# Scan preparation of an RWKV-7 layer with its log decays, normed keys and key factors kept in PSUM

## The chip, the cores and the metric

The kernel runs on one core of a Trainium2 chip. The metric is the device time of one execution in microseconds (us). A core has a matrix engine (TensorE, PE in the profile, with its weight loads as PEld), a vector engine (VectorE, DVE), a scalar engine (ScalarE, ACT), GpSimd (POOL), and SyncE (SP), which issues most DMAs. Matmul results land in PSUM, which is handled here as eight buffers (banks) of 512 fp32 columns on 128 partitions; all other tiles lie in SBUF. Each engine works through its own queue in order.

## The reference

Two sequences (256 and 1024 tokens, together T = 1280) run through two layers of width 1024. Layer 0 is a bidirectional RWKV-7 time mixer with 16 heads of 64, layer 1 neighbourhood attention; each is followed by a squared-ReLU MLP. The change touches only the inputs of the scan of layer 0:

```python
kk = _heads((k * k_k).astype(f32))
kk = kk * lax.rsqrt(jnp.maximum(jnp.sum(jnp.square(kk), axis=-1, keepdims=True), L2_EPS))
for d in range(2):
    w_lora = jnp.tanh(xw @ w1[d]) @ w2[d]
    decay = jnp.exp(-jnp.exp(-jax.nn.softplus(-(w0[d] + w_lora).astype(f32)) - 0.5))
    iclr = _heads(jax.nn.sigmoid((a0[d] + (xa @ a1[d]) @ a2[d]).astype(f32)))
    k_d = kf * (1.0 + (iclr - 1.0) * k_a_h)
    y = y + _wkv_scan(rf, _heads(decay), k_d, vf, -kk, kk * iclr, reverse=(d == 1))
    bonus = bonus + jnp.sum(rf * k_d * r_k, axis=-1, keepdims=True)
```

The log of the decay is -0.6065 times a sigmoid. `_wkv_scan` is computed later in chunks of 64 tokens. For each chunk it needs r, kk, k_d and kk*iclr multiplied by the exponential of the running sum of the log decays, or by its inverse.

## The kernel before

**Stages.** First the projections that give k and a part of r, then the stage of the change (about 315 to 677 us of the execution), then the scan of layer 0, its MLP, the attention layer and its MLP.

**Units.** The preparation has 48 units h: 8 blocks m of 128 channels (two heads), in each three segments of tokens (256, 512 and 512 wide), in each two directions d. So of six units in a row two are 256 wide and four are 512 wide, even units run forward and odd ones backward. For one unit:

- `prep_first` j = 0 and 1: a matmul of the decay's and of the rate's low-rank factors (`l<-tw,wa` and `l<-ta,wa`, L602), each followed by a tanh on ACT (L603), into `lw` and `tha`. j = 2: ACT's affine step makes the log decay of `lw` in place (L596). `lw` has 65 columns a chunk, one of which stays zero.
- `prep_scan`: DVE's scan (L615) sums the log decays within each chunk into `cs`; `prep_exp`: ACT makes exp(cs) and exp(-cs), `ec` and `emc` (L626, L629).
- `prep_keys`, even units only: a matmul spreads the inverse norms of the heads over the channels (`kb`, L675), DVE multiplies with the keys into `pkk` (L678).
- `prep_products`: POOL makes r*ec (L646) and kd*emc (L652); DVE makes the key factor 1+(iclr-1)*k_a out of `tha` (L648), multiplies it with k (L650, `kd`), and makes (tha+1)*kk (L654), -kk*ec (L656) and (tha+1)*kk*emc/2 (L658). L660 takes the decay of a whole chunk out of `ec`.
- `prep_store`: two DMAs on ACT's queue write the products to HBM.
- `prep_bonus`, for each pair of units: DVE multiplies kd with r (L690), PE sums over the head in `bps` (two columns a block of 128 tokens, L694), DVE copies that out (L696).

**Other work in the stage.** PE also projects the rest of r: 18 bursts of 24 matmuls into `rps` (L95 to L97, called from `rmm`), one for every two units from unit 7 on, evacuated by ACT. From unit 42 on it projects v (`vps`, L499 to L501), whose inputs are loaded and cast tile by tile (`vx`, `mh`, L430 and L431) from unit 39 on.

**Order.** The order of the compute engines is written out by hand: `at(t, f, ...)` puts a step at a time t, counted in units; the list is sorted by t and all is issued in that order, so that each engine's queue follows it. For unit h the matmul of `tw` stands at h-2.027, that of `ta` at h-2.13, the affine step at h-1.765, the scan at h-0.95, the products at h+0.084 to h+0.57, the bonus steps of an even unit at h+2.58, h+4.45 and h+5.824.

**PSUM.** Three buffers (`pa`) serve `rps` and `vps`; four (pool `ppl`, tag `l2`) are handed out in turn to the two matmuls of `prep_first` and to `kb`; one (pool `ppn`) is for `bps`. A matmul into a buffer waits until the last reader of what stood there is done.

Of the kernel before, what the change touches and what calls it, by code (L numbers as in the profile page):

```python
# [13 lines left out]
P = 128  # L14
# [4 lines left out]
L = 64  # L19
# [29 lines left out]
class Trunk:  # L49
# [50 lines left out]
    def l0_proj(self):  # L100
# [410 lines left out]
    def prep_open(self, bctx):  # L511
        nc, tc, a = self.nc, self.tc, self.a
        self.ar_d = self.dram("ar_d", [8, 2, P, 20, P])
        self.bk_d = self.dram("bk_d", [8, 2, P, 20, P])
        pp = self.pp = bctx.enter_context(tc.tile_pool(name="ppB", bufs=1, reuse_waits="tile", side="right"))
        self.pk = bctx.enter_context(tc.tile_pool(name="pkB", bufs=2, reuse_waits="tile", side="right"))
        self.ppl = bctx.enter_context(tc.tile_pool(name="plB", bufs=4, space=PSUM))
        self.ppn = bctx.enter_context(tc.tile_pool(name="pnB", bufs=1, space=PSUM))
        s = self.pre = {}
        for nm in ("tw", "ta"):  # L520
            s[nm] = pp.tile([P, T], F32, name=nm)

# [6 lines left out]
        nc.sync.dma_start(s["m65"], a["m65"])  # L529
        s["hw"] = pp.tile([P, 48], F32, name="hw")  # L530
        s["kr"] = pp.tile([96, 512], F32, name="kr")
        s["heads"] = pp.tile([96, 1024], F32, name="heads")
        nc.sync.dma_start(s["heads"], a["heads"][0:96])
        for i, (c0, c1) in enumerate(SEGS):
            nc.sync.dma_start(s["kr"][32 * i:32 * i + 16, :c1 - c0], self.scr["kr_d"][:, c0:c1])

    def prep_const(self):
        nc, s = self.nc, self.pre
        for d in range(2):
            for t in s["lw"][d]:  # L540
                nc.gpsimd.memset(t[:, :, 64 * d:64 * d + 1], 0.0)
# [45 lines left out]
    def prep_first(self, U, h, j):  # L587

        nc, pk, s, u = self.nc, self.pk, self.pre, U[h]
        m, d, c0, c1, w = self.prep_unit(h)  # L590
        c3 = lambda t: t[:, :w].rearrange("p (c j) -> p c j", j=L)
        lw = u["lw"] = s["lw"][d][h // 2 % 2]
        lv = lw[:, :w // L, 1 - d:65 - d]
        dr = slice(64 * d, 64 * d + 64)
        if j == 2:
            nc.scalar.activation(lv, lv, AF.Copy, scale=-0.5 * KAPPA, bias=-0.5 * KAPPA)  # L596
# [5 lines left out]
        nc.tensor.matmul(ps[:, :w], s["wa", m][dr, j, :], s[act][dr, c0:c1], start=True, stop=True)  # L602
        nc.scalar.activation(t, c3(ps), AF.Tanh, scale=0.5, bias=s["hw"][:, col + 8 * d + m:col + 8 * d + m + 1])  # L603

    def prep_scan(self, U, h):

        nc, pk, s, u = self.nc, self.pk, self.pre, U[h]
        m, d, c0, c1, w = self.prep_unit(h)
        nch = w // L
        flat = lambda t: t[:, :nch, :].rearrange("p c j -> p (c j)")  # L610
        cs = pk.tile([P, 8, 65], F32, name="cs", tag="cs")
        lf, cf = flat(u["lw"]), flat(cs)
        if d == 1:
            lf, cf = lf[:, ::-1], cf[:, ::-1]
        nc.vector.tensor_tensor_scan(out=cf, data0=s["m65"][:, :nch * 65], data1=lf, initial=0.0, op0=ALU.mult, op1=ALU.add)  # L615
        u["cs"] = cs

    def prep_exp(self, U, h, j):
        nc, pk, u = self.nc, self.pk, U[h]
        m, d, c0, c1, w = self.prep_unit(h)  # L620
        nch = w // L
        flat = lambda t: t[:, :nch, :].rearrange("p c j -> p (c j)")
        cs = u["cs"]
        if j == 0:
            ec = u["ec"] = pk.tile([P, 8, 65], F32, name="ec", tag="ec")
            nc.scalar.activation(flat(ec), flat(cs), AF.Exp)  # L626
        else:
            emc = u["emc"] = pk.tile([P, 512], F32, name="emc", tag="emc")
            nc.scalar.activation(emc[:, :w].rearrange("p (c j) -> p c j", j=L), cs[:, :nch, 1 - d:65 - d], AF.Exp, scale=-1.0)  # L629

    def prep_products(self, U, h, i):
        nc, pk, s, u = self.nc, self.pk, self.pre, U[h]
# [5 lines left out]
        tha, emc, ec = u["tha"][:, :w], c3(u["emc"][:, :w]), u["ec"]  # L638
# [6 lines left out]
        if i == 0:  # L645
            nc.gpsimd.tensor_tensor(out=ar[:, :nch, 64:128], in0=c3(r), in1=ec[:, :nch, 1 - d:65 - d], op=ALU.mult)  # L646
        elif i == 1:
            nc.vector.tensor_scalar(out=kd, in0=tha, scalar1=hw[:, 32 + m:33 + m], scalar2=hw[:, 40 + m:41 + m], op0=ALU.mult, op1=ALU.add)  # L648
        elif i == 2:
            nc.vector.tensor_tensor(out=kd, in0=kd, in1=k, op=ALU.mult)  # L650
        elif i == 3:
            nc.gpsimd.tensor_tensor(out=bk[:, :nch, 64:128], in0=c3(kd), in1=emc, op=ALU.mult)  # L652
        elif i == 4:
            nc.vector.scalar_tensor_tensor(out=tha, in0=tha, scalar=1.0, in1=kk, op0=ALU.add, op1=ALU.mult)  # L654
        elif i == 5:
            nc.vector.scalar_tensor_tensor(out=ar[:, :nch, 0:64], in0=c3(kk), scalar=-1.0, in1=ec[:, :nch, d:64 + d], op0=ALU.mult, op1=ALU.mult)  # L656
        elif i == 6:
            nc.vector.scalar_tensor_tensor(out=bk[:, :nch, 0:64], in0=c3(tha), scalar=0.5, in1=emc, op0=ALU.mult, op1=ALU.mult)  # L658
# [7 lines left out]
    def prep_keys(self, U, h, step):  # L666
# [4 lines left out]
            u["kk"] = U[h - 1]["kk"]  # L671
        elif step == 0:
            o = 32 * (h % 6 // 2)
            u["kb"] = self.ppl.tile([P, 512], F32, name="kb", tag="l2")
            nc.tensor.matmul(u["kb"][:, :w], s["heads"][o:o + 16, m * P:m * P + P], s["kr"][o:o + 16, :w], start=True, stop=True)  # L675
        else:
            u["kk"] = self.pk.tile([P, 512], F32, name="pkk", tag="pkk", bufs=2)
            nc.vector.scalar_tensor_tensor(out=u["kk"][:, :w], in0=u["k"][:, :w], scalar=self.v(V_KK, m), in1=u["kb"][:, :w], op0=ALU.mult, op1=ALU.mult)  # L678

    def prep_store(self, U, h, eng):  # L680
# [3 lines left out]
    def prep_bonus(self, U, h, step):  # L684
# [4 lines left out]
            kd = u["kd"][:, :w]  # L689
            nc.vector.scalar_tensor_tensor(out=kd, in0=kd, scalar=self.v(V_RK, m), in1=u["r"][:, :w], op0=ALU.mult, op1=ALU.mult)  # L690
        elif step == 1:
            u["pb"] = self.ppn.tile([P, 8], F32, name="bps", tag="bps")
            for b in range(nb):
                nc.tensor.matmul(u["pb"][:, 2 * b:2 * b + 2], u["kd"][:, b * P:(b + 1) * P], self.blk, start=True, stop=True)  # L694
        else:
# [1181 lines left out]
def host_layout(inputs):  # L1877
# [39 lines left out]
    m65 = np.ones((P, 8, 65), np.float32)  # L1917
    m65[:, :, 0] = 0
    o["lnx"] = np.stack([i["rw_lnx_g"][0].reshape(8, P), i["rw_lnx_b"][0].reshape(8, P)], 1)
    o["m65"] = m65.reshape(P, 520)  # L1920
    return {k: np.ascontiguousarray(v) for k, v in o.items()}


# [17 lines left out]
```

## Time and profile before

| what | value |
|---|---|
| median of 3 runs | 4277.6 us (4269.57 to 4279.12) |
| the profiled execution | 4272.5 us, its span 4270.5 us |
| mean granted clock of TensorE | 0.956 of full |
| busy over the span | PE 94%, DVE 61%, ACT 40%, POOL 37% |
| granted clock in 440 to 480 us | 0.74 |
| busy in 440 to 480 us | PE 37.60, DVE 35.90, ACT 18.70, POOL 26.00 us of 40 |
| granted clock in 1900 to 2000 us (first MLP) | 1.00, PE busy 100 us of 100 |

A busy share is the time in which an engine had an instruction under way. For PE it says little without the granted clock: at 0.50 the same matmul takes twice as long and counts twice. In the rows of a timeline, "x2" are the two records of one fp32 matmul of this stage. Idle time stands in brackets behind an instruction, with what ended it.

### The profile page before, as it was taken

The numbers are of one execution on the slowest core, as the hardware profiler recorded it, in microseconds if no ns is written. First come the engines' busy times: TensorE is split into PE (matmuls) and PEld (weight loads), VectorE is DVE, ScalarE is ACT, GpSimd is POOL, SyncE is SP. The second block draws the span as 40 slices with busy tenths as digits, with TensorE's granted clock in tenths as the row PEclk, the third lists the DMA queues.
The fourth block names the chain that finished last, engine by engine and source line by source line (L and its number), as shares of the span: only waits on it lengthen the run. The fifth ranks groups of instructions, "written<-read, shape, count | busy, mean of one in ns | idle before, by whom it ended". The sixth has DMA issues, their size and how long they took to land.

```text
span 4270.5 us, 69486 instructions
## 1 busy us (share of the span) xinstructions
PE 3994.8 (94%) x25060; PEld 3357.7 (79%) x25060; DVE 2623.4 (61%) x5253; ACT 1716.7 (40%) x4345; POOL 1582.1 (37%) x1877
## 2 busy tenths in 40 slices
PE   7888989888988879999999999999998999999999
PEld 4664658777887768788888888988777788888888
DVE  7888974567877765755555556046554755555555
ACT  6764442366766764211111113256664311111111
POOL 5446664133433353422222225044443422222222
PEclk8996779899999999999999999999999999999999
DMA  3334456566666534111111112535456111111111
GB/s 114 87 108 169 167 172 175 139 160 152 152 159 152 130 96 158 50 35 40 40 40 40 35 35 80 166 101 115 94 119 216 59 35 40 40 40 37 37 37 60
DMA packets 499864, 414.67 MB, mean 97 GB/s; under 512 B 290816, under 2 KB 401312, under 8 KB 499520
## 3 DMA queue, kind: packets, MB, share of 16 engines
q1 hardware_dynamic: 465104, 348.88, 29.5%
q10 hardware_dynamic: 34416, 61.35, 3.9%
q8 instruction: 197, 3.23, 0.3%
q14 instruction: 147, 1.20, 0.1%
HBM read 290.25 MB, written 125.83 MB: 97 GB/s over the span
## 4 chain that ended last, share of the span: by engine, by line
PE 64%; DVE 9%; ACT 3%; DMA 3%; issue 2%; POOL 1%; SPq 1%; ACTq 0%; DVEq 0%; POOLq 0%
PE ps L95 17%; PE ps L96 16%; PE ps L97 16%; DVE tmp L847 2%; DVE q L849 1%; DVE S L1036 1%; PE vps L499 1%; PE vps L501 1%; PE vps L500 1%; PE us L1028 1%; PE aps L807 1%; PE op L1856 1%; PE us L1015 1%; PE w L1006 1%; PE pt L1799 1%
## 5 line engine op out<-in xcount | busy, mean ns | idle before, releaser
L1402 DVE TENSOR_TENSOR x<-ps,x 128x256 f32<-128x256 f32 x1488 | 814.9, 596 | 644.2 <-PE ps L97 644.0
L95 PE MATMUL ps<-ah,whi 128*128 128x512 f32 (+1 forms) x2304 | 843.2, 366 | 0.0
L96 PE MATMUL ps<-al,whi 128*128 128x512 f32 (+1 forms) x2304 | 825.3, 358 | 0.0
L97 PE MATMUL ps<-ah,wlo 128*128 128x512 f32 (+1 forms) x2304 | 822.3, 357 | 1.8 <-DVE wlo L90 1.5
L90 POOL TENSOR_TENSOR wlo<-raw,whi 128x1024 fp32r<-128x1024 f32 (+1 forms) x178 | 390.7, 2195 | 837.3 <-ACT whi L89 833.6
L95 PE MATMUL ps<-hh,whi 128*128 128x512 f32 (+1 forms) x1536 | 547.2, 356 | 9.4 <-DVE x L1402 9.4
L96 PE MATMUL ps<-hl,whi 128*128 128x512 f32 (+1 forms) x1536 | 546.2, 356 | 0.0
L97 PE MATMUL ps<-hh,wlo 128*128 128x512 f32 (+1 forms) x1536 | 545.7, 355 | 0.0
L95 PEld LDWEIGHTS ps<-ah,whi 128*128 128x128 f32 x2304 | 434.3, 189 | 72.0 <-issue 7.8
L97 PEld LDWEIGHTS ps<-ah,wlo 128*128 128x128 f32 x2304 | 433.2, 188 | 72.8 <-DVE wlo L90 2.0
L96 PEld LDWEIGHTS ps<-al,whi 128*128 128x128 f32 x2304 | 434.5, 189 | 62.2 <-issue 1.0
L89 ACT CAST whi<-raw 128x1024 fp32r<-128x1024 f32 (+1 forms) x206 | 200.3, 972 | 703.1 <-PE ps L96 630.1
L1381 POOL TENSOR_TENSOR rl<-rl 128x512 f32<-128x512 f32 (+1 forms) x192 | 173.7, 905 | 505.9 <-PE ps L97 462.4
L1023 POOL COPY u<-hv 64x64 f32<-64x64 f32 x640 | 171.0, 267 | 457.9 <-ACT hv L1017 438.4
L95 PEld LDWEIGHTS ps<-hh,whi 128*128 128x128 f32 x1536 | 291.1, 190 | 53.8 <-DVE x L1402 11.4
L97 PEld LDWEIGHTS ps<-hh,wlo 128*128 128x128 f32 x1536 | 291.4, 190 | 41.7
L1380 ACT ACTIVATE rl<-ps 128x512 f32<-128x512 f32 (+1 forms) x192 | 100.7, 525 | 555.6 <-PE ps L97 555.6
L96 PEld LDWEIGHTS ps<-hl,whi 128*128 128x128 f32 x1536 | 291.1, 190 | 40.6
L1383 ACT CAST hh<-rl 128x512 fp32r<-128x512 f32 (+1 forms) x192 | 105.6, 550 | 324.0 <-POOL rl L1381 324.0
L1036 DVE SCALAR_TENSOR_TENSOR S<-us,dall,sd 64x64 f32<-64x64 f32 x512 | 144.6, 282 | 105.6 <-PE us L1028 97.4
L1384 DVE TENSOR_TENSOR hl<-rl,hh 128x512 fp32r<-128x512 f32 (+1 forms) x192 | 119.8, 624 | 143.2 <-ACT hh L1383 142.5
L1010 ACT COPY u<-w 64x64 f32<-64x64 f32 x640 | 130.8, 204 | 125.6 <-PE w L1006 115.2
(295 smaller groups left out, 8445.4 us busy)
## 6 DMA issues: line engine op xcount, KB each, us to landing
raw<-in_w_down_dram SPq DMA_DIRECT2D x64, 512.0 KB
raw<-in_w_up_dram SPq DMA_DIRECT2D x64, 512.0 KB
ar<-ar_d SPq DMA_DIRECT2D x80, 256.0 KB
bk<-bk_d SPq DMA_DIRECT2D x80, 256.0 KB
ar_d<-ar ACTq DMA_DIRECT2D x32, 512.0 KB
bk_d<-bk ACTq DMA_DIRECT2D x32, 512.0 KB
bs<-tab SPq DMA_DIRECT2D x128, 96.0 KB
v_d<-vt ACTq DMA_DIRECT2D x80, 128.0 KB
```

Of the source, the lines that this page charges most:

```text
L89: nc.scalar.copy(hi[:, cs], raw)
L90: lo_eng.tensor_tensor(out=lo[:, cs], in0=raw, in1=hi[:, cs].bitcast(F32), op=ALU.subtract)
L95: mm(ps, sh, mh, start=first, stop=False)
L96: mm(ps, sh, ml, start=False, stop=False)
L97: mm(ps, sl, mh, start=False, stop=last)
L1010: nc.scalar.copy(up[es, es], w[:64, es])
L1023: nc.gpsimd.tensor_copy(R["u2"][64 * e:64 * e + 64, 64 * e:64 * e + 64], J["hv"][0:64, cc, 64 * e:64 * e + 64])
L1036: nc.vector.scalar_tensor_tensor(out=S2[es, es], in0=sn[es, es], scalar=D, in1=R["sd"][es, es], op0=ALU.mult, op1=ALU.add)
L1381: nc.gpsimd.tensor_tensor(out=r[:, :n], in0=r[:, :n], in1=r[:, :n], op=ALU.mult)
L1383: nc.scalar.copy(hh[:, :n], r[:, :n])
L1384: nc.vector.tensor_tensor(out=hl[:, :n], in0=r[:, :n], in1=hh[:, :n].bitcast(F32), op=ALU.subtract)
L1402: nc.vector.tensor_tensor(out=xv, in0=ps[:, :n], in1=xv, op=ALU.add)
```

## The change

Log decays, the normed keys and the factor out of `ta` stay in PSUM. The matmul for the log decay writes `ltw`, the only buffer of pool `ppn`; tanh and the affine step work on it in place, and the scan reads it there, 64 columns a chunk instead of 65. `ec` takes over the 65th column, set to 1 once, in four lasting tiles. The matmul for the rate writes `lta` (two buffers); ACT puts the tanh into `tha` in SBUF as before, and one more ACT step (Identity with scale and offset) writes the key factor back to `lta`. DVE multiplies that with k, so that step 2 of the products falls away; then (tha+1)*kk overwrites `lta`. `kb` (two buffers) is overwritten with the normed keys and takes the place of `pkk`. `bps` shares the buffer of `ltw`. Four times in the list move: matmul and tanh of `ta` from h-2.13 to h-0.9, the scan from h-0.95 to h-1.2, the second and third bonus step to h+3.83 and h+3.94.

```diff
-            at(lead(-2.13), self.prep_first, U, h, 1)
+            at(lead(-0.9), self.prep_first, U, h, 1)
...
-            at(lead(-0.95), self.prep_scan, U, h)
+            at(lead(-1.2), self.prep_scan, U, h)
...
-                for i, t in enumerate((2.58, 4.45, 5.824)):
+                for i, t in enumerate((2.58, 3.83, 3.94)):
...
-        self.ppl = bctx.enter_context(tc.tile_pool(name="plB", bufs=4, space=PSUM))
+        self.ppl = bctx.enter_context(tc.tile_pool(name="plB", bufs=2, space=PSUM))
         self.ppn = bctx.enter_context(tc.tile_pool(name="pnB", bufs=1, space=PSUM))
...
-        if j == 1:
+        act, col, pool = (("tw", 0, self.ppn), ("ta", 16, self.ppl))[j]
+        ps = pool.tile([P, 512], F32, name="l" + act, tag="l" + act)[:, :w]
+        nc.tensor.matmul(ps, s["wa", m][dr, j, :], s[act][dr, c0:c1], start=True, stop=True)
+        bias = s["hw"][:, col + 8 * d + m:col + 8 * d + m + 1]
+        if j == 0:
+            u["lw"] = ps
+            nc.scalar.activation(ps, ps, AF.Tanh, scale=0.5, bias=bias)
+        else:
+            u["ta"] = ps
             u["tha"] = pk.tile([P, 512], F32, name="tha", tag="tha", bufs=3)
-        act, col, t = (("tw", 0, lv), ("ta", 16, j and c3(u["tha"])))[j]
-        ps = self.ppl.tile([P, 512], F32, name="l2", tag="l2")
-        nc.tensor.matmul(ps[:, :w], s["wa", m][dr, j, :], s[act][dr, c0:c1], start=True, stop=True)
-        nc.scalar.activation(t, c3(ps), AF.Tanh, scale=0.5, bias=s["hw"][:, col + 8 * d + m:col + 8 * d + m + 1])
+            nc.scalar.activation(u["tha"][:, :w], ps, AF.Tanh, scale=0.5, bias=bias)
+            nc.scalar.activation(ps, u["tha"][:, :w], AF.Identity, scale=s["hw"][:, 32 + m:33 + m], bias=s["hw"][:, 40 + m:41 + m])
...
-        nc.vector.tensor_tensor_scan(out=cf, data0=s["m65"][:, :nch * 65], data1=lf, initial=0.0, op0=ALU.mult, op1=ALU.add)
-        u["cs"] = cs
+        nc.vector.tensor_tensor_scan(out=cf, data0=s["m64"][:, :w], data1=lf, initial=0.0, op0=ALU.mult, op1=ALU.add)
...
         elif i == 1:
-            nc.vector.tensor_scalar(out=kd, in0=tha, scalar1=hw[:, 32 + m:33 + m], scalar2=hw[:, 40 + m:41 + m], op0=ALU.mult, op1=ALU.add)
+            nc.vector.tensor_tensor(out=kd, in0=ta, in1=k, op=ALU.mult)
         elif i == 2:
-            nc.vector.tensor_tensor(out=kd, in0=kd, in1=k, op=ALU.mult)
+            return
...
-            nc.vector.scalar_tensor_tensor(out=tha, in0=tha, scalar=1.0, in1=kk, op0=ALU.add, op1=ALU.mult)
+            nc.vector.scalar_tensor_tensor(out=ta, in0=tha, scalar=1.0, in1=kk, op0=ALU.add, op1=ALU.mult)
...
-            u["kk"] = self.pk.tile([P, 512], F32, name="pkk", tag="pkk", bufs=2)
+            u["kk"] = u["kb"]
...
-            u["pb"] = self.ppn.tile([P, 8], F32, name="bps", tag="bps")
+            u["pb"] = self.ppn.tile([P, 512], F32, name="bps", tag="ltw")
```

Two places show how the instructions move. PE, between the burst of `rps` that is 256 wide and the next one, before (`l<-ta` and `l<-tw` are the two matmuls of `prep_first`):

```order
L97 MATMUL rps<-mh_225,wl 128x256
L602 MATMUL l_3987<-ta,wa 128x512
L602 MATMUL l_3990<-tw,wa 128x512
L675 MATMUL kb<-kr,heads 128x512
L694 MATMUL bps<-cst,kd 128x2 x4
L602 MATMUL l_4023<-ta,wa 128x512
L602 MATMUL l_4028<-tw,wa 128x512
L95 MATMUL rps<-mh_184,wh 128x512
```

and with the change:

```order
L97 MATMUL rps<-mh_225,wl 128x256
L692 MATMUL bps<-cst,kd 128x2 x4
L597 MATMUL ltw<-tw,wa 128x512
L597 MATMUL lta<-ta,wa 128x512
L673 MATMUL kb<-kr,heads 128x512
L597 MATMUL ltw<-tw,wa 128x512
L597 MATMUL lta<-ta,wa 128x512
L95 MATMUL rps<-mh_184,wh 128x512
```

The sums of the bonus now stand first, and the matmul of `tw` ahead of that of `ta`; three of the six rows between the bursts write the one buffer of `ppn`.

DVE in the same place, with the change, from the copy of those sums to the next unit's normed keys (`kd<-lta` is the product with k, L652 to L656 the three other products, L688 the bonus product, `kb<-pk` the normed keys):

```order
L694 COPY bonus<-bps 128x4x2
L646 TENSOR_TENSOR kd<-lta,pk 128x512
L652 SCALAR_TENSOR_TENSOR lta<-tha,kb 128x512
L654 SCALAR_TENSOR_TENSOR ar<-kb,ec_3255 128x8x64
L656 SCALAR_TENSOR_TENSOR bk<-lta,emc 128x8x64
L688 SCALAR_TENSOR_TENSOR kd<-kd,vec,pr 128x256
L616 SCALAR_TENSOR_TENSOR cs<-m_3259,ltw 128x512
L676 SCALAR_TENSOR_TENSOR kb<-pk,vec,kb 128x512
```

The row L616 is the scan. The copy stands after a scan here, and ahead of the products of the next unit.

More of the change, by code (lines that the diff above doesn't have):

```diff
@@ L521, in prep_open @@
             s[nm] = pp.tile([P, T], F32, name=nm)
-        s["lw"] = [[pp.tile([P, 8, 65], F32, name=f"lw{d}{i}") for i in range(2)] for d in range(2)]
+        s["ec"] = [[pp.tile([P, 8, 65], F32, name=f"ec{d}{i}") for i in range(2)] for d in range(2)]
         s["raw"] = pp.tile([P, 640], F32, name="l2raw")
-        s["m65"] = pp.tile([P, 520], F32, name="m65")
+        s["m64"] = pp.tile([P, 512], F32, name="m64")
         for c0, c1 in SEGS:
@@ L528, in prep_open @@
                 nc.sync.dma_start(s[nm][:, c0:c1], self.scr[nm + "_d"][:, c0:c1])
-        nc.sync.dma_start(s["m65"], a["m65"])
+        nc.sync.dma_start(s["m64"], a["m64"])
         s["hw"] = pp.tile([P, 48], F32, name="hw")
@@ L539, in prep_const @@
         for d in range(2):
-            for t in s["lw"][d]:
-                nc.gpsimd.memset(t[:, :, 64 * d:64 * d + 1], 0.0)
+            for t in s["ec"][d]:
+                nc.gpsimd.memset(t[:, :, 64 * d:64 * d + 1], 1.0)
         for c0, c1 in SEGS:
@@ L620, in prep_exp @@
         m, d, c0, c1, w = self.prep_unit(h)
-        nch = w // L
-        flat = lambda t: t[:, :nch, :].rearrange("p c j -> p (c j)")
-        cs = u["cs"]
+        cs = u["cs"][:, :w]
         if j == 0:
-            ec = u["ec"] = pk.tile([P, 8, 65], F32, name="ec", tag="ec")
-            nc.scalar.activation(flat(ec), flat(cs), AF.Exp)
+            ec = u["ec"] = self.pre["ec"][d][h // 2 % 2]
+            nc.scalar.activation(ec[:, :w // L, 1 - d:65 - d], cs.rearrange("p (c j) -> p c j", j=L), AF.Exp)
         else:
             emc = u["emc"] = pk.tile([P, 512], F32, name="emc", tag="emc")
-            nc.scalar.activation(emc[:, :w].rearrange("p (c j) -> p c j", j=L), cs[:, :nch, 1 - d:65 - d], AF.Exp, scale=-1.0)
+            nc.scalar.activation(emc[:, :w], cs, AF.Exp, scale=-1.0)
     def prep_products(self, U, h, i):
@@ L637, in prep_products @@
         c3 = lambda t: t.rearrange("p (c j) -> p c j", j=L)
-        tha, emc, ec = u["tha"][:, :w], c3(u["emc"][:, :w]), u["ec"]
+        ta, tha, emc, ec = u["ta"], u["tha"][:, :w], c3(u["emc"][:, :w]), u["ec"]
         if "ar" not in u:
@@ L657, in prep_products @@
         elif i == 6:
-            nc.vector.scalar_tensor_tensor(out=bk[:, :nch, 0:64], in0=c3(tha), scalar=0.5, in1=emc, op0=ALU.mult, op1=ALU.mult)
+            nc.vector.scalar_tensor_tensor(out=bk[:, :nch, 0:64], in0=c3(ta), scalar=0.5, in1=emc, op0=ALU.mult, op1=ALU.mult)
         else:
@@ L1916, in host_layout @@
     o["heads"] = e.reshape(P, 1024)
-    m65 = np.ones((P, 8, 65), np.float32)
-    m65[:, :, 0] = 0
+    m64 = np.ones((P, 8, 64), np.float32)
+    m64[:, :, 0] = 0
     o["lnx"] = np.stack([i["rw_lnx_g"][0].reshape(8, P), i["rw_lnx_b"][0].reshape(8, P)], 1)
-    o["m65"] = m65.reshape(P, 520)
+    o["m64"] = m64.reshape(P, 512)
     return {k: np.ascontiguousarray(v) for k, v in o.items()}
```

13 lines of the change are left out of this document (4 added, 9 removed).

## The prediction

> **What bounds the kernel now.** Read the stretches first. One execution spans 4270.5 us and is timed at 4272.5; the change touches only the preparation of the scan, from about 315 to 677 us. The view of stretches, cut at the first and last matmul of `rps` (projection of r), gives for each stretch: length, then busy us and instruction counts of PE, PE's weight loads, DVE, ACT, POOL, then TensorE's granted clock. Its fourth row is the same middle stretch for the instructions on `rps` alone.
>
> ```profile
> 315.00:366.10 51.10, 34.73 (x62) 14.13 (x62) 41.01 (x52) 23.00 (x46) 28.39 (x27) 0.51 0.57 196
> 366.10:602.80 236.70, 223.56 (x716) 149.09 (x716) 208.44 (x260) 108.99 (x208) 155.53 (x133) 0.75 0.45 162
> 602.80:677.30 74.50, 57.02 (x303) 45.98 (x304) 57.80 (x65) 31.99 (x62) 52.57 (x45) 0.77 0.60 199
> 366.10:602.80 236.70, 120.59 (x432) 97.46 (x432) 7.95 (x16) 0.75 0.45 162
> ```
>
> In the middle PE is busy 94% and DVE 88%, so both are near their limit, and PE is there because its clock is granted at 0.75 only. Half of PE's time is `rps` (18 bursts, 120.6 us); the other 116.1 us are the 17 gaps between them, in which PE makes the small matmuls of the preparation. Next, the chain of waits: work of this stage lies on it, and DVE hands over to PE.
>
> ```profile
> 669.85 1.67 DVE ar L656
> 672.33 1.84 PE bps L694 x8
> ```
>
> So time gained or lost here moves the end one for one. Then PE's timeline (start, duration, "x" matmul passes, idle before). One gap of each kind follows: after the 256-wide burst, after the first 512-wide one, after the second.
>
> ```profile
> 452.94 1.12 PE L602 MATMUL l<-ta,wa 64*128 64x512 f32 x2
> 453.90 1.02 PE L602 MATMUL l<-tw,wa 64*128 64x512 f32 x2
> 455.90 1.05 PE L694 MATMUL bps<-cst,kd 128*128 128x2 f32 x8
> 456.88 1.12 PE L602 MATMUL l<-ta,wa 64*128 64x512 f32 x2
> 457.85 1.02 PE L602 MATMUL l<-tw,wa 64*128 64x512 f32 x2
> 458.80 0.73 PE L95 MATMUL rps<-mh,wh 128*128 128x512 f32 x1
> ...
> 466.06 0.70 PE L602 MATMUL l<-ta,wa 64*128 64x256 f32 x2
> 468.86 0.79 PE L694 MATMUL bps<-cst,kd 128*128 128x2 f32 x4 [1.05 <-DVE bonus L696]
> 469.58 1.22 PE L602 MATMUL l<-ta,wa 64*128 64x256 f32 x2
> 471.58 0.79 PE L95 MATMUL rps<-mh,wh 128*128 128x512 f32 x1
> ...
> 479.26 1.12 PE L602 MATMUL l<-ta,wa 64*128 64x512 f32 x2
> 483.67 1.87 PE L694 MATMUL bps<-cst,kd 128*128 128x2 f32 x8 [1.38 <-DVE bonus L696]
> 485.46 2.07 PE L602 MATMUL l<-ta,wa 64*128 64x512 f32 x2
> 487.33 1.91 PE L602 MATMUL l<-tw,wa 64*128 64x512 f32 x2
> 489.17 0.58 PE L95 MATMUL rps<-mh,wh 128*128 128x256 f32 x1
> ```
>
> The gaps last 458.80-452.94 = 5.86, 471.58-466.06 = 5.52 and 489.17-479.26 = 9.91 us. PE hardly waits in them: 0, 1.05 and 1.38 us. Start to start, a 512-wide `l` takes 0.96 us in the first and 1.85 in the third: the clock had halved. What halves it is seen by cutting at its steps:
>
> ```profile
> 455.50:458.90 3.40, 3.40 (x15) 1.74 (x13) 1.87 (x4) 2.44 (x5) 1.11 (x2) 1.00 0.41 154
> 458.90:462.30 3.40, 3.40 (x8) 2.64 (x9) 3.40 (x3) 1.05 (x3) 3.30 (x3) 0.50 0.01 2
> ```
>
> PE was busy all through 455.5-458.9, but with the small matmuls alone, and the next 3.4 us ran at 0.50. So small matmuls do not hold the clock; only `rps` does.
>
> **What the change makes cheaper.** DVE's share, from the groups kept apart by shape (busy us, mean ns):
>
> ```profile
> L656 DVE SCALAR_TENSOR_TENSOR ar<-pkk,ec 128x512 f32<-128x512 f32 x32 | 55.3, 1728 | 0.0
> L615 DVE TENSOR_TENSOR_SCAN cs<-m,lw 128x520 f32<-128x520 f32 x32 | 45.8, 1432 | 0.8 <-ACT lw L596 0.8
> L658 DVE SCALAR_TENSOR_TENSOR bk<-tha,emc 128x512 f32<-128x512 f32 x32 | 29.2, 912 | 0.0
> L648 DVE TENSOR_SCALAR kd<-tha,hw 128x512 f32<-128x512 f32 x32 | 25.3, 791 | 18.9 <-PE bps L694 18.9
> L650 DVE TENSOR_TENSOR kd<-kd,pk 128x512 f32<-128x512 f32 x32 | 24.3, 758 | 1.0
> L690 DVE SCALAR_TENSOR_TENSOR kd<-kd,vec,pr 128x512 f32<-128x512 f32 x16 | 23.5, 1471 | 1.1 <-POOL kd L664 1.1
> L690 DVE SCALAR_TENSOR_TENSOR kd<-kd,vec,pr 128x256 f32<-128x256 f32 x8 | 11.3, 1416 | 0.0
> L654 DVE SCALAR_TENSOR_TENSOR tha<-tha,pkk 128x512 f32<-128x512 f32 x32 | 23.0, 719 | 0.0
> L678 DVE SCALAR_TENSOR_TENSOR pkk<-pk,vec,kb 128x512 f32<-128x512 f32 x16 | 11.8, 735 | 0.0
> L678 DVE SCALAR_TENSOR_TENSOR pkk<-pk,vec,kb 128x256 f32<-128x256 f32 x8 | 3.8, 470 | 14.3 <-PE kb L675 14.3
> L696 DVE COPY bonus<-bps 128x8 f32<-128x8 f32 x16 | 2.5, 154 | 10.1 <-PE bps L694 10.1
> L615 DVE TENSOR_TENSOR_SCAN cs<-m,lw 128x260 f32<-128x260 f32 x16 | 11.7, 729 | 1.7 <-issue 1.7
> ...
> L615 DVE TENSOR_TENSOR_SCAN cs<-m,lw x48: 681/1227/2299, 321.4 to 657.3; 128x520 f32<-128x520 f32 x32, 128x260 f32<-128x260 f32 x16
> ```
>
> A 512-wide unit costs DVE 1432+791+758+719+1728+912 = 6.34 us, and each second unit also 735+1471+154, so 7.52 us on average. The change drops L648 and gives scan, key product and the three products an operand in PSUM. The one DVE operation of this stage that reads PSUM already is L678, 735 ns; the same form with both inputs in SBUF takes 719 to 1728. I price the four products at 735 (470 when 256 wide), and the scan, 8 columns shorter, at 1250, near the 1227 that is the median over both widths in the row of its line (min/median/max, ns) and under its mean of 1432. Bounds: 0.72 us a product (L654) and, a loss, 1.73 (L656). Writing to PSUM from DVE is in no row. The sum is 1.25+4x0.735+1.18 = 5.37 us, 2.15 less a unit, 0.71 of before.
>
> What ACT gains: one Identity a unit, reading SBUF, writing PSUM. It is priced as the affine step of the log decay, beside its tanh:
>
> ```profile
> L603 ACT ACTIVATE tha<-l,hw 128x512 f32<-128x512 f32 x32 | 22.0, 686 | 77.6 <-DVE bk L658 43.5 <-DVE bonus L696 20.1 <-PE l L602 13.9
> L596 ACT ACTIVATE lw<-lw 128x512 f32<-128x512 f32 x32 | 20.2, 632 | 5.1 <-ACT lw L603 1.4 <-POOL ml L431 1.4 <-POOL ar L646 0.5
> ```
>
> 48 times 0.63 us on an engine busy 109 of 237 us would cost nothing by itself; it counts because it now stands in the chain below. POOL and the DMAs keep their instructions. The decay's edge columns become a memset to 1 in four tiles, nothing in time.
>
> **What it makes dearer: one bank.** Before, `l` rotated through four buffers and PE could run ahead. Now `ltw` has one buffer, held from its matmul over tanh and affine step until DVE's scan has read it, and the bonus sums `bps` use that same buffer. So PE's order in a gap becomes: `bps`; wait for DVE's copy; `ltw`; `lta`; `kb`; wait for DVE's scan; `ltw`; `lta`; next `rps`. Behind the waiting second `ltw` the whole `rps` burst is queued. Between the two waits run, one after the other, `ltw` and `lta` (PE), tanh, Identity and affine step (ACT, which takes the second matmul's tanh and Identity ahead of the affine step), and the scan; beside them DVE must do four products and the bonus product L690, which keeps two SBUF inputs (1.47, or 1.42 when 256 wide; 1.47 is used throughout), ahead of the scan. Price of a gap, with 0.05 us for a handover, `bps` and the first two matmuls at full clock as right after `rps` in the rows above, the last two at half clock:
> - after the 256-wide burst: `bps` 0.98, copy with handovers 0.25, then DVE 4x0.735+1.47 = 4.41 (PE and ACT meanwhile 0.96+1.00+0.69+0.63+0.63+0.05 = 3.96), scan 1.25, handover 0.05, `ltw` 1.87, `lta` 1.84: 10.65, that is 4.8 more;
> - after the first 512 one: 0.72+0.25+4.41+0.73+0.05+(471.58-469.58 = 2.00) = 8.16, 2.6 more;
> - after the second: 0.98+0.25+(4x0.470+1.47 = 3.35)+1.25+0.05+3.71 = 9.59, 0.3 less.
>
> Six, six and five such gaps: 28.8+15.6-1.5 = **+43 us**. In the other half of each pair of units nothing new binds: the scan ends some 5.2 us after `ltw` (1.84+0.69+0.63+0.63+1.25 and handovers) while PE works on `lta` and `rps`.
>
> The Trainium skill says otherwise of the half clock: its page "TensorE: Matmul & The Clock Gate", section "Why this matters for your kernels", has the clock fall after a stretch of PE idleness of about 3 us and asks that gaps stay under that. By that rule the new idle time (about 2.8 us at most) would leave the clock full and the sum would be the second rival's. The trace disagrees: busy with small matmuls for a whole 3.4 us, PE still dropped to 0.50.
>
> **Start and tail.** Before the first `rps` there are some four pairs of units at clock 0.51. A 512-wide unit needs one pass of the bank: 1.87+1.87+0.69+0.63+0.63+1.25+0.15 = 7.1 us, each second one also 1.79+0.25 for `bps`: 16.2 us a pair against DVE's 2x7.52 = 15.0 today. Four pairs: **+5** (0 to 9, since the first units also fill the chain). In the tail PE waits for DVE, and DVE for casts that wait for loads:
>
> ```profile
> 614.77 1.87 PE L694 MATMUL bps<-cst,kd 128*128 128x2 f32 x8 [7.80 <-DVE bonus L696]
> L430 ACT CAST mh<-vx 128x512 fp32r<-128x512 f32 x16 | 9.9, 618 | 16.3 <-DMA vx<-vm_d 16.3
> ```
>
> Those loads stay, so the cheaper DVE counts only in the last three units behind them: 3x2.15, **-7** (0 if the loads still decide; at most the 74.5-57.0 = 17.5 us in which PE idles there). Sum: 43+5-7 = +41, 4313.5 against the profiled execution's 4272.5. That execution lies 5.1 us under the median of 4277.6, so I forecast **4319 us**.
>
> **The rivals.**
> - *PE gets its work sooner and the stage shrinks* (chance 0.10). If DVE were what holds PE (88% busy, and the 18.9 us in the L648 row fall away with the earlier `bps`), and PE's waits for the scan were short, the middle would shrink to PE's 223.6 busy us: -13; start 0.29x41 = -11; tail -9. That gives 4245. It decides where the chain between the two waits takes less than PE's `ltw`, `lta` and `kb`, some 3 us; against it stand six operations of 0.6 to 1.5 us in series.
> - *The matmuls ahead of `rps` stay at full clock* (0.17). The first gap above kept it for all of its 5.86 us, the third lost it after 4. If it holds, each gap loses 1.8, 0.9 and 1.8 us against my prices: increments 3.0, 1.7 and -2.1, middle +18, total +16, 4294 us.
> - *PSUM costs DVE dearly* (0.08). At the bound of 1.73 a product, DVE ahead of the scan takes 4 us longer in two gaps of three, 2 in the third: some 55 us more, 4375.
> - *It all cancels* (0.03): no gap grows, because waits for the scan only replace idle time that was there. The rows leave 0, 1.05 and 1.38 us for that.
>
> **How the numbers follow.** My forecast has 0.62. Its own range is 4303 to 4344: from start 0 and tail -17.5, to start 9, tail 0 and half of what it would add if the first matmuls of a gap too ran at half clock (2.1, 0.9 and 1.9 us a gap, 28 in all). The range of 8 in 10 leaves out the first and third rival and takes in the second with its start at 0 and its tail at -17.5, and the whole of the 28: 4279 to 4358. About 0.2% (9 us) is what a measurement can tell here. Faster: 0.10. Within it: 0.03 and the low edge of the second rival, 0.04. Slower: the rest, 0.83.
>
> **What would show it.** Right: the stretch with `rps` lengthens from 236.7 to about 280 us, `rps` itself stays near 120; before each second `ltw` PE idles 2 to 3 us with DVE's scan as releaser; granted clock in that stretch at or under 0.75; DVE busy there falls from 208 to about 150; L648's successor and the products sit near 0.74 us. Wrong: PE idles less than a microsecond ahead of `ltw`, or the clock rises over 0.8, or a DVE product with a PSUM operand is over 1 us.

## The result and the profile after

The changed kernel takes 4282.4 us (median of 13 runs, 4276.67 to 4288.01) against 4273.8 (13 runs, 4268.03 to 4279.12) on the same chip: 1.0019 times as long, interval 1.0011 to 1.0027, or 8.6 us. It is slower, as forecast, but by a fifth of the 41 us that the sum had. Ratios, here and below, are those of the fast runs with their 95% interval and differ by up to 0.001 from the quotient of the two medians given. Its profiled execution spans 4279.1 us, 8.6 more than the one of before, so the two can be compared directly.

The stretches of the changed kernel, cut as before at the first and last matmul of `rps` (length, then busy us and instructions of PE, PE's weight loads, DVE, ACT, POOL, then the granted clock); the last row is the middle for `rps` alone (PE, weight loads, ACT):

```profile
315.00:372.70 57.70, 29.20 (x60) 10.22 (x60) 31.02 (x51) 27.18 (x54) 21.68 (x27) 0.51 0.53 184
372.70:618.20 245.50, 183.59 (x719) 121.16 (x717) 137.82 (x232) 133.41 (x253) 120.14 (x141) 0.78 0.46 165
618.20:677.30 59.10, 41.13 (x229) 32.48 (x230) 25.98 (x43) 28.93 (x53) 25.40 (x28) 0.80 0.47 159
372.70:618.20 245.50, 109.82 (x432) 88.32 (x432) 8.47 (x17) 0.78 0.46 165
```

The middle grew from 236.7 to 245.5 us, 8.8 and not 43. It has two parts that moved against each other: `rps` itself fell from 120.6 to 109.8 us, and the gaps between its bursts grew from 236.7-120.6 = 116.1 to 245.5-109.8 = 135.7, by 19.6. PE is busy 183.6 us where it was 223.6. So PE now waits, and its work got cheaper at the same time.

What PE waits for in the middle, before and after (us in all, times, longest):

```profile
PE bps L694 <- DVE bonus L696: 13.1, 11, 2.1
```

```profile
PE ltw L597 <- DVE cs L616: 55.2, 17, 10.7
...
PE bps L692 <- DVE cs L616: 2.3, 5, 1.1
```

The first row is the wait that the prediction priced: before the second `ltw` of each of the 17 gaps, DVE's scan as releaser, (55.2-10.7)/16 = 2.8 us each but for the last.

Where the cheaper work comes from stands in PE's timeline, in the same gap that the change's order shows (start, duration, "64*128" the rows and columns of the weights, idle before):

```profile
460.75 0.69 PE L597 MATMUL ltw<-tw,wa 64*128 64x512 f32 x1 [0.26 <-DVE bonus L694]
460.76 0.69 PE L597 MATMUL lta<-ta,wa 64*128 64x512 f32 x1
...
466.08 1.22 PE L597 MATMUL ltw<-tw,wa 64*128 64x512 f32 x1 [3.15 <-DVE cs L616]
466.09 1.22 PE L597 MATMUL lta<-ta,wa 64*128 64x512 f32 x1
467.09 1.06 PE L597 MATMUL ltw<-tw,wa 64*128 64x512 f32 x1
...
468.09 0.79 PE L95 MATMUL rps<-mh,wh 128*128 128x512 f32 x1
```

Each row is one of the two passes of an fp32 matmul, and the passes of `ltw` and `lta` start within 0.01 us of each other: the two run **at the same time**. From 466.08 the pair takes 468.09-466.08 = 2.01 us up to the next `rps`, at half clock. In the rows of before, `l<-ta` starts at 485.46 and `l<-tw` only at 487.33, and both together take 3.71.

Why now and not before: these matmuls use 64 rows, `dr = slice(64*d, 64*d + 64)`, the lower or the upper half by the direction d of the unit. Before, the matmuls of `tw` and `ta` of one unit stood side by side (h-2.027 and h-2.13): same d, same rows. With `ta` at h-0.9 the neighbour of `tw` of unit h is `ta` of unit h-1, which has the other direction, and so the other half of the rows.

Between the two waits, on DVE and on ACT of the changed kernel:

```profile
463.13 0.47 DVE L688 SCALAR_TENSOR_TENSOR kd<-kd,vec,pr 128x256 f32<-128x256 f32 x1
464.80 1.22 DVE L616 TENSOR_TENSOR_SCAN cs<-m,ltw 128x512 f32<-128x512 f32 x1 [1.20 <-ACT ltw L593]
...
461.97 0.66 ACT L601 ACTIVATE ltw<-ltw,hw 128x512 f32<-128x512 f32 x1 [2.79 <-PE lta L597]
...
463.27 0.78 ACT L606 ACTIVATE lta<-tha,hw 128x512 f32<-128x512 f32 x1
464.19 0.58 ACT L593 ACTIVATE ltw<-ltw 128x512 f32<-128x512 f32 x1
```

DVE is through with its products at 463.6 and then idles 1.20 us for ACT's affine step: the longer of the two branches is ACT's, not DVE's. DVE's groups over the stage, by shape (busy us, mean ns, idle before):

```profile
L616 DVE TENSOR_TENSOR_SCAN cs<-m,ltw 128x512 f32<-128x512 f32 x32 | 39.0, 1220 | 59.9 <-ACT ltw L593 59.9
L652 DVE SCALAR_TENSOR_TENSOR lta<-tha,kb 128x512 f32<-128x512 f32 x32 | 22.2, 695 | 1.0
L654 DVE SCALAR_TENSOR_TENSOR ar<-kb,ec 128x512 f32<-128x512 f32 x32 | 21.9, 683 | 0.0
...
L646 DVE TENSOR_TENSOR kd<-lta,pk 128x512 f32<-128x512 f32 x32 | 21.8, 681 | 0.0
L688 DVE SCALAR_TENSOR_TENSOR kd<-kd,vec,pr 128x512 f32<-128x512 f32 x16 | 13.8, 860 | 0.4 <-POOL kd L662 0.4
```

The four products sit at 0.68 to 0.70 us and the bonus product fell from 1.47 to 0.86. DVE's work came out slightly below its price, and what it saves beyond the end of ACT's branch was worth nothing by itself, since DVE idles 59.9 us for `ltw`.

### The profile page after: what moved, and what is told of

Read it like the earlier page. It is cut to its first block, busy times and chain, and to the rows that moved or that the text cites. A ratio compares the mean times of both kernels' runs of the same rounds, so it can differ in the third digit from the quotient of the medians.

```text
span 4279.1 us, 69428 instructions
## 1 busy us (share of the span) xinstructions
PE 3938.5 (92%) x25060; PEld 3317.0 (78%) x25060; DVE 2513.1 (59%) x5205; ACT 1746.4 (41%) x4393; POOL 1523.3 (36%) x1877
## 4 chain that ended last, share of the span: by engine, by line
PE 68%; DVE 14%; ACT 5%; DMA 5%; issue 4%; POOL 2%; SPq 2%; ACTq 0%; DVEq 0%; POOLq 0%
PE ps L95 17%; PE ps L96 17%; PE ps L97 16%; DVE tmp L845 2%; DVE q L847 2%; DVE S L1034 1%; PE vps L499 1%; PE vps L501 1%; PE vps L500 1%; PE us L1026 1%; PE aps L805 1%; PE ltw L597 1%; PE op L1854 1%; DVE mu L182 1%; PE us L1013 1%
## 5 line engine op out<-in xcount | busy, mean ns | idle before, releaser
L95 PE MATMUL ps<-ah,whi 128*128 128x512 f32 (+1 forms) x2304 | 842.4, 366 | 0.0
L97 PE MATMUL ps<-ah,wlo 128*128 128x512 f32 (+1 forms) x2304 | 823.0, 357 | 1.8 <-DVE wlo L90 1.5
L95 PE MATMUL ps<-hh,whi 128*128 128x512 f32 (+1 forms) x1536 | 547.4, 356 | 9.5 <-DVE x L1400 9.5
L97 PE MATMUL ps<-hh,wlo 128*128 128x512 f32 (+1 forms) x1536 | 545.4, 355 | 0.0
L95 PEld LDWEIGHTS ps<-ah,whi 128*128 128x128 f32 x2304 | 434.4, 189 | 72.0 <-issue 7.8
L97 PEld LDWEIGHTS ps<-ah,wlo 128*128 128x128 f32 x2304 | 433.2, 188 | 72.4 <-DVE wlo L90 2.0
L95 PEld LDWEIGHTS ps<-hh,whi 128*128 128x128 f32 x1536 | 291.0, 189 | 53.8 <-DVE x L1400 11.4
L97 PEld LDWEIGHTS ps<-hh,wlo 128*128 128x128 f32 x1536 | 291.4, 190 | 41.7
```

The lines of the kernel that those rows point to most:

```text
L95: mm(ps, sh, mh, start=first, stop=False)
L97: mm(ps, sl, mh, start=False, stop=last)
```

## The experiments

**Is it the rows?** In the first run the halves of `ta` and of its weights are exchanged, so that the neighbours `ltw` and `lta` share their rows again; order, waits and banks stay those of the change.

```diff
-            for nm in ("tw", "ta"):
-                nc.sync.dma_start(s[nm][:, c0:c1], self.scr[nm + "_d"][:, c0:c1])
+            nc.sync.dma_start(s["tw"][:, c0:c1], self.scr["tw_d"][:, c0:c1])
+            for o in (0, 64):
+                nc.sync.dma_start(s["ta"][o:o + 64, c0:c1], self.scr["ta_d"][64 - o:128 - o, c0:c1])
...
-        dr = slice(64 * d, 64 * d + 64)
+        dr = slice(64 * (d ^ j), 64 * (d ^ j) + 64) if j < 2 else None
```

(The weights `wa2` are loaded with the same exchange.)

> The changed kernel with the halves of the rate's low-rank inputs and weights exchanged (rows 0 to 63 now hold direction 1), so that the two small matmuls that stand next to each other on PE use the same half of the array's rows; all else as in the changed kernel, but for a few more loads at the start and one or two more DMA issues per block of channels. Theory (rows): in the changed kernel ltw and lta of neighbouring units lie on different halves of the rows and run at the same time, which the prediction had in series; with the same half they go in series again: a pair takes about 1.9 us at full clock and 3.7 at half, where it took 1.1 and 2.0, the rps bursts together rise from 110 towards 120 us, and the time rises by 35 to 55 us over the changed kernel, to 4317 to 4337. Rival (cheaper DVE): the prediction was off since DVE's products and the bonus product became shorter than priced; then the time stays within 6 us of the changed kernel's 4282. Rival (clock): the pairs stay short in cycles and only the granted clock differs.

Measured: 4331.79 us (4321.71 to 4336.39) against 4275.75, ratio 1.0135 (1.0115 to 1.0155), some 49 us over the changed kernel. PE's timeline, its stretch, the stretch for `rps` alone and its wait:

```profile
471.93 2.07 PE L600 MATMUL ltw<-tw,wa 64*128 64x512 f32 x2 [3.50 <-DVE cs L619]
473.80 1.91 PE L600 MATMUL lta<-ta,wa 64*128 64x512 f32 x2
475.64 0.58 PE L95 MATMUL rps<-mh,wh 128*128 128x256 f32 x1
...
380.20:665.30 285.10, 230.53 (x717) 147.77 (x717) 137.73 (x230) 135.81 (x253) 118.65 (x138) 0.70 0.40 143
380.20:665.30 285.10, 118.46 (x432) 96.72 (x432) 8.46 (x17) 0.70 0.40 143
...
PE ltw L600 <- DVE cs L619: 50.2, 17, 10.8
```

The pair is in series again, 475.64-471.93 = 3.71 us up to the next `rps`. The wait for the scan is about as long as in the changed kernel (50.2 against 55.2 us), the stretch is 39.6 us longer: PE is busy 46.9 us more. So the difference is PE's own work, not its waits. This is also the kernel that the prediction had in mind: it had a stretch of "about 280" and `rps` "near 120", and here are 285.1 and 118.5; its time is 13 us above the 4319 and inside the forecast's own range. The time expected of the rows, 4317 to 4337, came out.

**The same exchange on the kernel before**, where it does the opposite: there it puts neighbours of one unit into different halves. It adds the same loads.

> The kernel before with the same exchange of halves: there the two small matmuls of one unit stood next to each other on the same half of the rows; now they lie on different halves. Theory (rows): each pair shrinks by 0.9 us at full and 1.8 at half clock, 17 gaps have two pairs; DVE, busy 208 of 237 us in that stretch, is the next limit, so the stretch from the first to the last rps falls from 237 to between 212 and 228 and the time by 8 to 25 us, to 4249 to 4266. Rival (DVE holds PE): the time stays within 4 us of the kernel before and PE idles more instead.

Measured: 4265.35 us (4262.18 to 4274.09), ratio 0.9978 (0.9968 to 0.9987), some 10 us faster, at the edge of what was expected.

```profile
367.10:595.50 228.40, 185.24 (x717) 126.72 (x715) 214.95 (x263) 109.34 (x211) 159.29 (x134) 0.81 0.48 171
367.10:595.50 228.40, 107.43 (x432) 87.56 (x432) 7.96 (x16) 0.81 0.48 171
...
PE bps L697 <- DVE bonus L699: 43.1, 14, 5.3
```

PE's work falls here too, from 223.6 to 185.2 us, but DVE is busy 215.0 of 228.4, and PE's wait for it grows from 13.1 to 43.1. So with the pairs in parallel the kernel before is bound by DVE, which the change relieves.

**Is it the bank?** The log decay goes back to a tile in SBUF, written by the tanh, so that the one buffer of `ltw` is free after the tanh and not after the scan. All else of the change stays.

```diff
-            u["lw"] = ps
-            nc.scalar.activation(ps, ps, AF.Tanh, scale=0.5, bias=bias)
+            u["lw"] = pk.tile([P, 512], F32, name="lw", tag="lw", bufs=3)[:, :w]
+            nc.scalar.activation(u["lw"], ps, AF.Tanh, scale=0.5, bias=bias)
```

> The changed kernel with the log decay back in SBUF: tanh writes an SBUF tile, so that the one bank of ltw is free after tanh and not after the scan. Theory (bank held over the scan is what the changed kernel waits for): PE's 84 us of waits before ltw for the scan fall below 25, the stretch from first to last rps falls from 245 to 205 to 225 us, and the time to 4245 to 4265, under both kernels; the scan is back to some 1.4 us, since both its inputs lie in SBUF. Rival (something else, ACT's chain or the loads, would hold PE just as long): the time stays at 4275 to 4285 and the wait before ltw has another releaser.

Measured: 4219.08 us (4216.65 to 4222.31), ratio 0.9874 (0.9856 to 0.9891). It beats both kernels, the one before by some 55 us, and was faster than the theory had it.

```profile
457.83 0.69 PE L597 MATMUL ltw<-tw,wa 64*128 64x512 f32 x1
...
358.60:563.20 204.60, 178.53 (x719) 117.25 (x717) 149.06 (x236) 133.53 (x253) 132.45 (x142) 0.84 0.57 201
358.60:563.20 204.60, 103.47 (x432) 83.02 (x432) 8.33 (x17) 0.84 0.57 201
...
PE ltw L597 <- DVE bonus L694: 17.2, 17, 3.4
...
L616 DVE TENSOR_TENSOR_SCAN cs<-m,lw 128x512 f32<-128x512 f32 x32 | 47.0, 1468 | 16.0 <-ACT lw L593 16.0
```

No idle time stands before the second pair any more, the wait for the scan is gone from PE's list (the 84 us of the expectation are those of the whole stage, 55.2 of them in the middle), and the stretch is 40.9 us shorter than with the change. DVE does more here than there (149.1 against 137.8 us; the scan, with both inputs in SBUF, is back at 1.47 us): that the scan reads PSUM saves DVE 0.25 us a unit and costs PE a wait of 2.8 us a gap.

**Shorter queue behind the wait.** Each `rps` burst is halved, the second twelve matmuls one unit later, so that less stands behind a waiting `ltw`.

```diff
-                at(6 * m + 2 * s - RL, rmm, m, s)
+                at(6 * m + 2 * s - RL, rmm, m, s, 0)
+                at(6 * m + 2 * s - RL + 1.0, rmm, m, s, 1)
```

(`rmm` then loops over 4 of the 8 steps of k; the evacuation stands at +1.9 instead of +1.4.)

> The changed kernel with each rps burst cut in two halves of 12 matmuls, the second half a unit later, ahead of the second ltw of the gap instead of behind it. Theory (bank wait): PE has rps work in the time in which the bank waits for ACT and the scan; idle time of PE before ltw falls from 84 us to 20 to 45 and the time to 4250 to 4270. Rival (the bank's own round of matmul, three ACT steps and scan is the limit, twice in every pair of units): PE idles as long in sum, with more of it ahead of bps, and the time stays within 8 us of 4282.

Measured: 4270.36 us (4264.59 to 4278.68), ratio 0.9995 (0.9985 to 1.0005): 12 us less than the change and no different from before. The time is at the upper end of what was expected, 4270, and the reason holds only by half.

```profile
370.00:615.30 245.30, 206.98 (x732) 128.84 (x731) 141.84 (x235) 138.30 (x263) 125.00 (x146) 0.78 0.49 175
...
PE bps L695 <- DVE cs L619: 25.9, 14, 3.2
PE ltw L600 <- DVE cs L619: 7.8, 4, 3.7
```

The wait for the scan falls from 57.5 us (the rows of `ltw` and of `bps`, 55.2 and 2.3) to 33.7, and most of what is left moved to `bps`, which shares the buffer. But `rps` is now busy 119.7 us instead of 109.8, and the stretch is as long as with the change (245.3). The 12 us lie outside of it: `rps` starts 2.7 us earlier, the first `vps` comes at 615.1 instead of 621.3, and the projection of v then takes 157.4 us instead of 165.1. Why it does was not followed.

**Are the normed keys in PSUM worth their bank?** The normed keys go back to a tile in SBUF.

```diff
-            u["kk"] = u["kb"]
+            u["kk"] = self.pk.tile([P, 512], F32, name="pkk", tag="pkk", bufs=2)
```

> The changed kernel with the normed keys back in SBUF, so that two of DVE's products, (tha+1)*kk and -kk*ec, read two SBUF operands again, as before. Theory: these two take 0.9 to 1.7 us when POOL is at work and 0.69 when not, as before the change, against 0.68 to 0.70 in all executions of the changed kernel; they stand ahead of the scan on which PE waits, but ACT's three steps there end about 1.2 us later than DVE's products, so that less than half of it is seen: 4282 to 4298. Rival (cheaper DVE gave back what the prediction missed): at least 20 us more than the changed kernel, 4302 or above.

Measured: 4290.36 us (4283.08 to 4295.97) against 4271.52, ratio 1.0042 (1.0027 to 1.0056); some 10 us are lost to the change's own 1.0019. DVE's product of keys and `ec`, as a group and in time beside POOL:

```profile
L654 DVE SCALAR_TENSOR_TENSOR ar<-pkk,ec 128x512 f32<-128x512 f32 x32 | 44.2, 1382 | 0.5 <-DMA ar_d<-ar 0.5
...
459.83 1.72 POOL L650 TENSOR_TENSOR bk<-kd,emc 128x512 f32<-128x512 f32 x1 [1.50 <-DVE kd L646]
460.34 1.75 DVE L654 SCALAR_TENSOR_TENSOR ar<-pkk,ec 128x512 f32<-128x512 f32 x1
```

L654 doubles, from 0.683 to 1.382 us in the mean, and here both it and POOL's product beside it take about 1.7 us. L652, which reads two SBUF operands in this run too, rose in the mean only from 0.695 to 0.736; here it began at 459.73, ahead of POOL's product, and kept its 0.70 us. POOL's product at the same place of the changed kernel, where L654 takes 0.68:

```profile
461.43 1.27 POOL L650 TENSOR_TENSOR bk<-kd,emc 128x512 f32<-128x512 f32 x1 [1.49 <-DVE kd L646]
```

The keys and the log decay are thus on opposite sides: one is better in PSUM and the other is not.

**Halved bursts on the better kernel** (the edits of the third and fourth run together).

> The log decay in SBUF as in the fastest kernel so far (4219 us) and the rps bursts in two halves. Theory (the bank no longer makes PE wait in the gaps, so there is little for the halves to fill): 4212 to 4228, with the waits of ltw for DVE's copy not longer than before. Rival (splitting gains its 12 us again): 4200 to 4211.

Measured: 4226.04 us (4223.33 to 4226.87), ratio 0.9888 (0.9874 to 0.9903): within what was expected and no gain over 0.9874. Without the wait there is nothing for it to shorten.

**Rows and bank together**: the exchange of the first run on the better kernel.

> The log decay in SBUF and the exchanged halves, so that neighbouring small matmuls share rows and go in series. Theory (rows): PE, busy 36 of 40 us in that kernel's middle stretch, has 17 times two pairs at 0.9 to 1.8 us more to do and rps bursts at a later rise of the clock: 25 to 60 us more than 4219, 4244 to 4279. Rival (in series they cost only where the bank makes PE wait): within 8 us of 4219.

Measured: 4261.23 us (10 runs, 4244.59 to 4270.81), ratio 0.997 (0.9956 to 0.9985), some 41 us over the better kernel. PE is busy in all but 12 us of the stretch, so this again is its own work:

```profile
366.10:613.20 247.10, 234.73 (x718) 149.51 (x717) 144.13 (x232) 135.76 (x252) 126.21 (x141) 0.70 0.46 165
366.10:613.20 247.10, 124.99 (x432) 101.53 (x432) 8.33 (x17) 0.70 0.46 165
...
L95 PE MATMUL rps<-mh,wh x144: 387/415/794, 366.1 to 612.4; 128*128 128x512 f32 x96, 128*128 128x256 f32 x48
```

In the last row (min/median/max ns), no matmul of line L95 takes less than 387 ns, so that none of its 48 that are 256 wide ran at full clock, where one takes 0.28 us; in the changed kernel the same row begins at 277. (Among those of L97 the shortest took 281, so that a few at the end of a burst did.)

Together: with the pair in series, the kernel before, the change and the better kernel take 1, 1.0135 and 0.997 of the time before; with the pair in parallel 0.9978, 1.0019 and 0.9874. By the differences, the rows are worth 9, 50 and 41 us in the three kernels; the bank of the log decay costs 70 us in series and 62 in parallel, much the same; and what the better kernel has besides (less work for DVE, but also the new order and one more ACT step, which no run takes apart) is worth 13 us in series and 44 in parallel: in series PE is busy 234.7 of 247.1 us, which leaves little to gain from the other engines.

## Why the prediction was right in sign and wrong in size

**The step that failed** is the last one of each gap's price, "`ltw` 1.87, `lta` 1.84". It took PE's matmuls to run one after the other, as they do in the rows of before. In the changed kernel the second pair takes 2.01 us after the 256-wide burst, as shown; after the first and the second 512-wide burst:

```profile
479.31 0.48 PE L597 MATMUL ltw<-tw,wa 64*128 64x256 f32 x1 [2.20 <-DVE cs L616]
...
479.94 0.50 PE L95 MATMUL rps<-mh,wh 128*128 128x512 f32 x1
...
493.46 1.22 PE L597 MATMUL ltw<-tw,wa 64*128 64x512 f32 x1 [2.94 <-DVE cs L616]
...
495.47 0.58 PE L95 MATMUL rps<-mh,wh 128*128 128x256 f32 x1
```

These are 0.63 us (256 wide) and 2.01. Against the prices of 3.71, 2.00 and 3.71 that is, over six, six and five gaps, 6x1.70+6x1.37+5x1.70 = 27 of the 43 us. In the second kind of gap most of this is the clock: the pair was priced at half clock and ran at full, where two in series take 467.12-466.06 = 1.06 us in the kernel before (`kb` follows at 467.12), so 0.94 of the 1.37. In the first run, with the rows shared, the pairs take just what was priced, 3.71, 2.00 and 3.71. The gaps grew by 19.6, 23.4 less than priced: 27 less by the pairs, some 8 more in the last gap (below), and some 4 less in the rest, above all behind the first 512-wide burst, where the second `ltw` starts 479.31-475.36 = 3.95 us after the first instead of 4.41+0.73+0.05 = 5.19. The new order as printed shows the neighbours, and the diff shows `dr`; what was not asked is which rows neighbours use. The Trainium skill states the rule, in "TensorE: Matmul & The Clock Gate", section "Part 3: Packing small matmuls — row/col tiling": matmuls in different row groups of the array overlap, with starts some 4 ns apart. The trace agrees (0.01 us apart, its last digit).

**"`rps` itself stays near 120"** failed with it: 109.8. The sentence "small matmuls do not hold the clock; only `rps` does" was read from pairs in series. In the clock records of all nine traces every low stretch of the middle lasts 3.41 us or a multiple of it, at 0.50, so here the clock changes in steps of that length. Below are the step that holds the start of a 256-wide burst and the one behind it, first in the changed kernel, then in the first run, which differs from it in the rows (columns as above):

```profile
575.98:579.39 3.41, 3.41 (x12) 1.91 (x11) 1.55 (x5) 1.72 (x3) 1.93 (x4) 0.50 0.32 102
579.39:582.80 3.41, 3.14 (x26) 2.85 (x24) 1.22 (x1) 1.97 (x4) 1.17 (x1) 1.00 0.41 154
```

```profile
521.93:525.35 3.42, 3.42 (x11) 1.92 (x11) 0.00 (x0) 2.21 (x4) 0.72 (x2) 0.50 0.24 85
525.35:528.76 3.41, 3.41 (x17) 3.41 (x17) 1.22 (x1) 1.50 (x3) 1.18 (x1) 0.50 0.39 143
```

Both first steps are at half clock with PE busy throughout: some 1.55 us of `ltw` and `lta`, then `rps` for 1.85 and 1.87. Behind the matmuls in parallel the next step has the full clock, behind those in series the half. So here the pair that fills all 128 rows counted towards the rise, and the one in series did not. Of all such steps with 1.4 to 2.0 us of `rps`, in the seven kernels with whole bursts, none of 19 with the pair in series was followed by full clock, and all of 12 with the pair in parallel were; with less `rps` the parallel ones vary. Where a step begins within a burst differs from burst to burst, so the gain is one in the mean: the clock rises 1.8 to 4.3 us after a burst's start in the changed kernel, 2.8 in the mean, and 3.4 to 5.4 before, 4.1 in the mean. The totals bear it out: 120.6, 118.5 and 125.0 us of `rps` in the three kernels with the pair in series (before, first and seventh run), 107.5, 109.8 and 103.5 in their counterparts with the pair in parallel. That makes the 10.8 us by which the bursts shrank. No run isolated what the clock alone is worth in the whole kernel: the exchange changes the pair's time and the clock together.

**Smaller misses in the middle.** Of the part between the two waits the price was DVE's four products, L690 at 1.47 and the scan; it is ACT's two tanh, Identity and affine step and then the scan instead, as DVE's idle time of 1.20 us shows, and it lasts 466.08-460.75 = 5.33 us against 5.71. Identity cost 0.78 us, not 0.63, the affine step in PSUM 0.58. The last gap is a miss of its own:

```profile
604.95 1.53 DVE L431 TENSOR_TENSOR ml<-vx,mh 128x256 fp32r<-128x256 f32 x1 [2.92 <-ACT mh L430]
...
610.38 0.79 PE L597 MATMUL ltw<-tw,wa 64*128 64x256 f32 x1 [10.65 <-DVE cs L616]
```

There the scan stands on DVE's queue behind a product that waits for casts of `vx`, and through the one bank this wait reaches PE: 10.65 us, some 8 over the others.

**What held.** The bank wait is there in every gap, with the releaser named and at 2.8 us for "2 to 3". The first `rps` comes at 372.7 instead of 366.1: +6.6 for "+5 (0 to 9)". The net of everything behind the middle is 8.6-6.6-8.8 = -6.8 for "-7", an agreement that is partly luck, since it has other parts than the cheaper DVE: the first `vps` comes 3.1 us after the last `rps` and not 13.7, which is 10.6 gained, and the projection of v gives some of it back (the stretches, after and before, from its first to its last matmul):

```profile
621.30:786.40 165.10, 144.71 (x1085) 137.23 (x1084) 54.66 (x109) 48.12 (x97) 47.84 (x49) 0.91 0.52 153
```

```profile
616.50:776.00 159.50, 147.76 (x1083) 139.40 (x1083) 73.59 (x115) 44.04 (x90) 56.17 (x48) 0.92 0.54 158
```

DVE is busy 137.8 us in the middle for "about 150"; the granted clock, 0.78, is just over the 0.75 that was to be its limit, which goes with the earlier rise in the bursts. PSUM was not dear for DVE, 0.68 to 0.70 against the price of 0.735, so the rival at 4375 us is out. The rival at 4245, by which PE gets its work sooner and the stage shrinks, is out for the change and comes true in the better kernel, at 4219. None of the prediction's own signs of being wrong appeared (2.8 us of waiting, a clock of 0.78, products of 0.70): none of them looked at the pairs.

**The rival at 4294** (matmuls ahead of `rps` at full clock) came nearest in number, for a reason that is not the measured one: the second pair of a gap runs at 1.22 and 1.06 us a pass after 3.15 us of idle time, twice the 0.69 and 0.59 of the first pair. Its claim on the clock failed after two bursts of three, behind waits of 3.15 and 2.94 us, and held after the first 512-wide one, behind 2.20; and the pair was cheap above all by running in parallel. What halves the clock there stays open: the idle time or the want of full matmuls, which come together in this kernel (in the kernel before it halved without idle time, as the prediction's rows show).

Why did only the products with two SBUF inputs vary, and the bonus product get cheaper though the change doesn't touch it? In the fifth run L654 doubles beside POOL once both inputs lie in SBUF. The Trainium skill says so in "SBUF — State Buffer", section "Who interferes with whom": a DVE instruction with two SBUF inputs contends with a GpSimd instruction that reads SBUF, one with at most one, outside the modes that use two ports, doesn't. The trace agrees, 1.38 against 0.683 us for L654. With four products out of POOL's way there is less contention left for the bonus product too, 0.86 against 1.47; that last step is argued, not tested.

## What to carry to other kernels

When a change reorders matmuls that use part of the array's rows, look at which rows the new neighbours use before adding up their times: here the same matmuls cost 3.71 or 2.01 us a pair, and the clock of the burst behind them moved too. An operand held in PSUM costs the time for which its bank stays taken, so ask who queues behind the next writer: the normed keys were worth some 10 us there, the log decay cost over 60. A branch that stops being the longer one (DVE's here) is worth nothing more until the wait it feeds is gone, and then all of it may come at once.

## What was not expected of the hardware

- Two fp32 matmuls of 64 rows each, 512 wide, in opposite halves of the rows take 2.01 us together at half clock, 3.71 in the same half; so the second is nearly free.
- A PE that is busy throughout a step of 3.41 us need not get the full clock in the next: with one 64-row matmul of a pair in series ahead of 1.87 us of full ones it did not, with two side by side ahead of 1.85 us it did.
- An ACT step of 512 columns from SBUF into PSUM (Identity with a scale and an offset for each partition) took 0.78 us, the affine one within PSUM 0.58.
- A DVE product with one operand in PSUM and one in SBUF hardly varies (min/median/max ns over both widths, changed kernel), where it took 1.75 us with both in SBUF in the fifth run's row above:

```profile
L654 DVE SCALAR_TENSOR_TENSOR ar<-kb,ec x48: 417/683/684, 328.3 to 674.1; 128x512 f32<-128x512 f32 x32, 128x256 f32<-128x256 f32 x16
```
